# Attention probabilities left unnormalised; reciprocal row sums go through DRAM as rows and scale the z gates on GpSimd

## The chip, the core and the metric

The kernel runs on one core of a Trainium2 chip. The metric is the device time of one execution in microseconds. A core has these engines, each with a queue of its own that it works through in order: TensorE (PE in the profile, PEld for its weight loads), VectorE (DVE), ScalarE (ACT), GpSimd (POOL) and SyncE (SP). SP, ACT and POOL also issue the DMA transfers; a DMA that has to wait for something waits on its engine's queue, and all that stands behind it there waits too.

## What is computed

Two layers of a hybrid trunk over 512 tokens behind 16 learned meta tokens, 1024 channels wide. Each layer has a pooling branch and an attention branch with 8 heads of 96 query and 64 value channels. Only the attention branch is touched. Cut to that:

```
q, k, v  = projections of the layer's input, normalised, with rotary positions
s        = q @ k.T / sqrt(96), causal
p        = softmax(s)
o        = p @ v
y_mla    = (o * silu(z_mla)) @ mla_w_up
x        = x + (sigmoid(g_pool) * y_pool + sigmoid(g_mla) * y_mla) @ w_out
```

`silu(z_mla)` multiplies `o` element by element, so a factor that belongs to a query row of a head can stand on `p`, on `o`, or on the gate of z.

## The kernel before

Activations stand with channels on partitions and tokens along the free axis, `[128, 528]` a tile (16 meta tokens, then 512). Each product of float32 matrices is made of three matmuls in a faster format: weights and activations are split into a high and a low part, and high by high, high by low and low by high are summed (`mm3`, lines 188, 191, 192). The split of a weight tile is one ScalarE and one VectorE instruction (`wload`, lines 183 and 184: `whi`, `wlo`).

The main stream of weight products is a generator (`stream`), advanced by `step`. The attention heads are written between its pieces: `fill` and `gap` let so many nanoseconds of the stream pass by an own clock, and `after(ns, fn)` puts a piece of work off until that clock has gone on by `ns`; `LAG` is 2000. From this program order the scheduler of the build makes the order on each engine. So a change at one head moves instructions of the stream against those of the heads.

One head in `go` consists of these steps.

- `prep` makes its keys. VectorE multiplies the one half (line 849), POOL the other (line 850, `tmp<-kp,bc`); then `split` makes `kh` on ScalarE (line 297) and `kl` on VectorE (line 298). Part of the queries is made by lines 856 and 857.
- `head` makes the scores of four blocks of 128 queries in PSUM (`S`), takes their maximum on VectorE (line 879), and the exponentials with their row sums `rs` on ScalarE (line 886). Lines 918 and 919 finish the sum of the longest block and take the reciprocals. Then POOL multiplies the exponentials by these, for each of four blocks the 16 meta columns into `pm` (line 924) and the others in place (line 926), in `pa` and two `cq` tiles.
- `pv`, called for the head before, transposes the probabilities on PE (line 946, against the identity `cst`), splits them into `th` and `tl`, and multiplies by the values into `o` (lines 951 and 952). Two heads make a pair. At a pair's second head the meta columns of both are split on ScalarE and VectorE (lines 939 to 941, `pmr`) and transposed (line 957, against `identr`), and ScalarE copies that to `racc` (line 960).
- `part2`, put off by `2 * LAG` (3 for the last pair), adds the meta tokens' part by a matmul (line 974, `racc` by `vb`), multiplies by the z gate (line 982 in the first layer, a line like it in the last), and splits the result into `ogs`, the input of the products with `mla_w_up` (`mu`).

A layer's heads run beside the gates' weight products. POOL also issues accumulating DMAs that add up pairs of weight tiles for later (`weight_sums`, line 353, `wsum` and `wsumgp`), some of them between the heads. The z gates `zms` stand in `u` tiles. `tmp` is a pool of three buffers that almost all short-lived results share, among them the first stage of the gates (line 715) and the sum over a pair of heads, which keeps one until `part2` is through.

Of the kernel before, what the change touches and what calls it, by code (L numbers as in the profile page):

```python
# [9 lines left out]
F32 = mybir.dt.float32  # L10
# [3 lines left out]
AF = mybir.ActivationFunctionType  # L14
# [4 lines left out]
P = 128  # L19
DEPTH = 2  # L20
D = 1024
SEQ = 512
NM = 16
T = SEQ + NM
# [16 lines left out]
MT_ZM = 24  # L41
MT_GM = 28

C_ID, C_MASK = 0, 128
C_IK, C_IR = 256, 272
C_KPE, C_CQ = 284, 292
C_MM, C_VBD, C_INVF, C_CNT = 300, 316, 324, 325
N_CONST = 389

G_H, G_CKV, G_CQ, G_QN, G_QR, G_KN, G_KR, G_PS = 0, 8, 10, 16, 17, 18, 19, 20  # L50
# [4 lines left out]
LAG = 2000.0  # L55
# [17 lines left out]
def trunk(ctx, tc, xT, pos, win, wkr, wqb, wkb, wvb, wgr, wpu, wmu, wout, gains, const, yT):  # L73
# [26 lines left out]
    def mmt():  # L100
        return pp.tile([P, 512], F32, tag="mm", name=nm("mm"), bufs=4)
# [4 lines left out]
    FULL = [(0, HALF), (HALF, T)]  # L106
    XTOK = [(NM, T)]

    cst = cp.tile([P, N_CONST], F32, name="cst")
    gn = cp.tile([P, DEPTH * N_GAIN], F32, name="gn")  # L110
    xb = cp.tile([P, 8, W], F32, name="xb")
    early = []
# [17 lines left out]
    act.activation(warm, warm, AF.Copy)  # L130
    posb = slot("u3", I32)
    ident = cst[:, C_ID:C_ID + P]
    ones = cp.tile([P, P], F32, name="ones")
    dve.memset(ones, 1.0)
    wps = pp.tile([P, 512], F32, tag="o", name="wps", bufs=1)
    for i in range(WARM):
        pe.matmul(wps[:, 0:P], ones, ones, start=True, stop=True)
    maskw = cp.tile([P, 512], BF16, name="maskw")
    gp.memset(maskw[:, :512 - P], 0.0)
    identr = cp.tile([P, P], F32R, name="identr")  # L140

    def other_loads(made):
        for k, m in ((2, 0), (4, 1), (6, None)):
            ins = sp.dma_start(xb[:, k:k + 2, :T], xT[:, k:k + 2, :])
            behind(ins, made)
            if m is not None:
                raw = rawt()
                behind(sp.dma_start(raw, win[0, MT_CKV + m, :, 512:1024]), made)
                early.append(raw)
        behind(sp.dma_start(cst, const), made)  # L150
        behind(sp.dma_start(posb[:, :T], pos.partition_broadcast(P)), made)
        dve.tensor_copy(maskw[:, 512 - P:], cst[:, C_MASK:C_MASK + P])
        dve.tensor_copy(identr, ident)

    tcos, tsin = slot("tc")[:, :T], slot("ts")[:, :T]
# [105 lines left out]
    def after(ns, fn):  # L261
        pend.append((clk[0] + ns, fn))
        pend.sort(key=lambda e: e[0])
# [32 lines left out]
    def split(hi, lo, src, a, b):  # L296
        act.activation(hi[:, a:b], src, AF.Copy)  # L297
        dve.tensor_sub(lo[:, a:b], src, hi[:, a:b].bitcast(F32))  # L298
# [28 lines left out]
    scr = dp.tile([P, 8, SEQ], F32, name="scr")  # L327
    ndr = [[dp.tile([1, T], F32, name=f"ndr{l}{i}") for i in range(2)] for l in range(DEPTH)]
    ksr = [dp.tile([H, T], F32, name=f"ksr{l}") for l in range(DEPTH)]
    kdr = [dp.tile([H, T], F32, name=f"kdr{l}") for l in range(DEPTH)]  # L330

    wsum = {n: [dp.tile([P, 4, 512], F32, name=f"wsum{n}{u}") for u in range(k)] for n, k in (("gp", 4), (0, 2), (1, 2))}
# [26 lines left out]
    class Layer:  # L359
# [503 lines left out]
        def head(self, h, kq, prev, between):  # L863
            kh, kl, qh, ql = kq
            odd = h % 2
            nqs, hold = self.nqs, h == 0
            pa = slot("pa", bufs=2, w=416)
            pb = slot(f"cq{8 + odd}")
            pc = slot(f"cq{10 + odd}")
            bia = sm.tile([P, 5], F32, tag="bia", name=nm("bia"), bufs=2)  # L870
            rs = sm.tile([P, 5], F32, tag="rs", name=nm("rs"), bufs=2)

            def scores(i, out, a, b):
                q0 = NM + P * i
# [12 lines left out]

            pt = [pa[:, 0:144], pa[:, 144:416], pb[:, 0:400], pc[:, 0:T]]
            sa = sct()
            s1, s3 = sa[:, 0:272], sa[:, 272:272 + SPL]  # L890
            scores(1, s1, 0, 272)
            scores(3, s3, 0, SPL)
            top(1, 1, s1, causal(272))
            top(3, 4, s3, maskw[:, 0:SPL])
            sb = sct()
            s2 = sb[:, 0:400]
            scores(2, s2, 0, 400)
            if not self.last:
# [12 lines left out]
            scores(0, s0, 0, 144)  # L911
            top(3, 3, s4, causal(T - SPL))
            top(0, 0, s0, causal(144))
            dve.tensor_tensor(out=bia[:, 3:4], in0=bia[:, 3:4], in1=bia[:, 4:5], op=ALU.min)
            expo(3, 4, s3, pt[3][:, 0:SPL])
            expo(3, 3, s4, pt[3][:, SPL:T])
            expo(0, 0, s0, pt[0])
            dve.tensor_add(rs[:, 3:4], rs[:, 3:4], rs[:, 4:5])
            dve.reciprocal(rs[:, 0:4], rs[:, 0:4])  # L919
            if odd == 0:  # L920
                self.pm = sm.tile([P, 4, 32], F32, tag="pm", name=nm("pm"), bufs=2)
            for i in range(4):
                n = pt[i].shape[1]
                gp.tensor_mul(self.pm[:, i, 16 * odd:16 * odd + 16], pt[i][:, 0:NM],  # L924
                              rs[:, i:i + 1].to_broadcast([P, NM]))
                gp.tensor_mul(pt[i][:, NM:], pt[i][:, NM:], rs[:, i:i + 1].to_broadcast([P, n - NM]))  # L926
            return h, pt, self.pm

        def pv(self, prev, js):
            if prev is None:  # L930
                return
            h, pt, pm = prev
# [9 lines left out]
            for j in js:  # L942
                n = SEQ - P * j
                tr = mmt()
                for i in range(j, 4):
                    pe.transpose(tr[:, P * (i - j):P * (i - j + 1)], pt[i][:, NM + P * j:NM + P * (j + 1)], ident)  # L946
# [20 lines left out]
            dve.tensor_add(op, ops[n0:n0 + 64, :], op)  # L967
            if odd == 1:
                op = self.op
                mt = self.mt  # L970

                def part2():
                    th, m = mt, mmt()
                    pe.matmul(m, self.vb[:, P * p:P * (p + 1)], th[0:96, 0:512], start=True, stop=True)
                    self.ogs[p] = (slot(f"q{p}", F32R), slot(f"kn{p}", F32R))
                    f = op[:, NM:T]
                    dve.tensor_add(f, m, f)
                    if self.last:
                        dve.scalar_tensor_tensor(out=f, in0=f, scalar=0.5, in1=self.zms[p][:, NM:T],
                                                 op0=ALU.mult, op1=ALU.mult)  # L980
                    else:
                        dve.tensor_mul(f, f, self.zms[p][:, NM:T])
                    split(*self.ogs[p], f, NM, T)

                after((3 if p == 3 else 2) * LAG, part2)

        def meta_queries(self):
            smeta = self.smeta
            mxm = sm.tile([NM, 8], F32, tag="mxm", name=nm("mxm"))
# [404 lines left out]
```

## Time and profile before

| | us |
|---|---|
| median of 3 runs | 786.61 |
| lowest, highest | 786.53, 788.80 |
| the profiled execution | 785.38 |
| its span in the profile | 783.4 |

The span goes from the first instruction to the last; the execution's time has some 2.0 us more around it. Layer 0's heads lie at about 190 to 330 us of the span, layer 1's at 590 to 720. In the rows below, `out<-in` are the program's tiles without their numbers, `x` stands ahead of a count, and a group's row has its busy time, the mean of one in nanoseconds, and the idle time of its engine just before it with what ended it. Rows of the timeline begin with the start and the length in microseconds. In rows of the waits, the numbers are the total, the times and the longest. Rows of DMAs have the size of one and the median time from its issue until it has landed.

### The profile page before, as it was taken

The page shows a single profiled execution, that of the slowest core. Times are in us where ns is not written, and L with a number is a line of the kernel's source. Part 1 is how long each engine was busy: PE and PEld are TensorE (multiplying, and loading weights), DVE is VectorE, ACT ScalarE, POOL GpSimd, SP SyncE. Part 2 cuts the span into 40 slices and gives each one's busy share as a digit, 9 for nine tenths or more (in the row PEclk, how much of TensorE's full clock was granted, in tenths as well). Part 3 has the DMA queues.
Part 4 walks back from the last instruction along what each step waited for, and adds up shares of the span by engine and source line. Part 5 has one row for each costly group of instructions (what it writes and reads, how often), then busy time and mean ns, then how long its engine had stood idle before and what let it go on. Part 6 is the DMA issues. An engine that isn't in the chain of part 4 may idle for free.

```text
span 783.4 us, 15391 instructions
## 1 busy us (share of the span) xinstructions
PE 774.6 (99%) x5493; PEld 712.5 (91%) x5493; DVE 592.2 (76%) x1329; ACT 443.6 (57%) x1007; POOL 222.5 (28%) x310
## 2 busy tenths in 40 slices
PE   9999999999999999999999999999999999999998
PEld 8999899999999999999997898887788999887887
DVE  5848788447778977689875487775998899874995
ACT  8645645645556665544654356555657676764451
POOL 1024515203434332211110145131016334440211
PEclk9999999999999999999999999999999999999999
DMA  6242357765645465565533422425446666562751
GB/s 244 82 100 86 104 156 172 178 159 134 145 121 137 120 136 146 135 185 168 167 108 95 96 88 87 134 88 168 135 129 162 167 164 169 154 221 74 225 166 68
DMA packets 63005, 109.16 MB, mean 139 GB/s; under 512 B 10368, under 2 KB 14592, under 8 KB 62928
## 3 DMA queue, kind: packets, MB, share of 16 engines
q1 hardware_dynamic: 54640, 89.76, 38.1%
q0 software_dynamic: 7280, 16.59, 11.3%
q10 hardware_dynamic: 1008, 1.84, 0.6%
q8 instruction: 43, 0.70, 0.4%
q14 instruction: 34, 0.28, 0.1%
HBM read 100.18 MB, written 22.62 MB: 157 GB/s over the span
## 4 chain that ended last, share of the span: by engine, by line
PE 86%; DVE 5%; DMA 5%; issue 2%; ACT 1%; POOL 0%; ACTq 0%; DVEq 0%
PE mm L188 25%; PE mm L192 24%; PE mm L191 24%; PE S L191 2%; PE S L192 2%; PE S L188 2%; PE mm L946 2%; DVE wlo L184 2%; PE o L952 1%; PE o L951 1%; DMA raw<-wsumgp 1%; PE S L500 1%; DMA raw<-win 1%; PE mm L402 1%; DMA wsum<-wsum 1%
## 5 line engine op out<-in xcount | busy, mean ns | idle before, releaser
L188 PE MATMUL mm<-hh,whi 128*128 128x264 f32 (+2 forms) x1000 | 306.9, 310 | 1.1 <-DVE tmp L637 0.6
L191 PE MATMUL mm<-hl,whi 128*128 128x264 f32 (+2 forms) x1000 | 305.4, 307 | 0.0
L192 PE MATMUL mm<-hh,wlo 128*128 128x264 f32 (+2 forms) x1000 | 305.2, 308 | 0.2 <-DVE wlo L184 0.2
L184 DVE TENSOR_TENSOR wlo<-raw,whi 128x512 fp32r<-128x512 f32 (+2 forms) x261 | 189.4, 729 | 92.0 <-ACT whi L183 88.0
L183 ACT ACTIVATE whi<-raw 128x512 fp32r<-128x512 f32 (+2 forms) x261 | 156.3, 602 | 157.8 <-PE mm L191 93.0
L188 PEld LDWEIGHTS mm<-hh,whi 128*128 128x128 f32 x1000 | 187.5, 188 | 11.9 <-DVE tmp L637 0.8
L191 PEld LDWEIGHTS mm<-hl,whi 128*128 128x128 f32 x1000 | 188.2, 188 | 8.8
L192 PEld LDWEIGHTS mm<-hh,wlo 128*128 128x128 f32 x1000 | 187.2, 188 | 9.3 <-DVE wlo L184 1.2
L188 PE MATMUL mm<-cq,whi 128*128 128x264 f32 (+2 forms) x156 | 48.6, 312 | 0.9 <-ACT whi L183 0.9
L192 PE MATMUL mm<-cq,wlo 128*128 128x264 f32 (+2 forms) x156 | 48.0, 310 | 0.6 <-DVE wlo L184 0.6
L191 PE MATMUL mm<-cq,whi 128*128 128x264 f32 (+2 forms) x140 | 43.4, 311 | 0.0
L879 DVE CUSTOM_DVE_ANT_0 S<-S,maskw,nqs 128x288 f32<-128x288 f32 (+4 forms) x80 | 38.4, 496 | 2.5 <-PE S L192 2.2
L702 POOL TENSOR_TENSOR racc<-racc,tmp 128x264 f32<-128x264 f32 (+1 forms) x15 | 14.2, 948 | 85.1 <-ACT tmp L701 85.0
L188 PE MATMUL mm<-u,whi 128*128 128x264 f32 (+1 forms) x108 | 35.3, 326 | 0.1
L192 PE MATMUL mm<-u,wlo 128*128 128x264 f32 (+1 forms) x108 | 34.8, 322 | 0.0
L298 DVE TENSOR_TENSOR tl<-mm,th 128x512 fp32r<-128x512 f32 (+1 forms) x64 | 29.2, 480 | 7.3 <-ACT th L297 6.2
L850 POOL TENSOR_TENSOR tmp<-kp,bc 64x528 f32<-64x528 f32 x16 | 25.8, 1614 | 28.0 <-issue 13.7
L926 POOL TENSOR_TENSOR cq<-cq,rs 128x384 f32<-128x384 f32 (+1 forms) x32 | 33.4, 1043 | 0.0
L353 POOL DMA_DIRECT2D wsum<-wout x8 | 6.9, 863 | 89.2 <-PE mm L192 83.8
L188 PEld LDWEIGHTS mm<-cq,whi 128*128 128x128 f32 x156 | 29.4, 188 | 2.6 <-ACT whi L183 1.1
L192 PEld LDWEIGHTS mm<-cq,wlo 128*128 128x128 f32 x156 | 29.4, 188 | 2.6 <-DVE wlo L184 1.1
L924 POOL TENSOR_TENSOR pm<-pa,rs 128x16 f32<-128x16 f32 x32 | 11.4, 357 | 70.6 <-DVE rs L919 64.8
(342 smaller groups left out, 1699.7 us busy)
## 6 DMA issues: line engine op xcount, KB each, us to landing
raw<-win SPq DMA_DIRECT2D x139, 256.0 KB, 3.0
raw<-wout SPq DMA_DIRECT2D x22, 256.0 KB, 3.3
bc<-kdr SPq DMA_DIRECT2D x16, 264.0 KB, 4.2
wsum<-wout SPq DMA_DIRECT2D x16, 256.0 KB, 3.5
raw<-wpu SPq DMA_DIRECT2D x16, 256.0 KB, 3.2
wsumgp<-win SPq DMA_DIRECT2D x16, 256.0 KB, 3.3
raw<-wmu SPq DMA_DIRECT2D x16, 256.0 KB, 2.7
raw<-wsumgp SPq DMA_DIRECT2D x16, 256.0 KB, 3.5
```

The lines of the kernel that those rows point to most:

```text
L183: act.activation(hi[:, :n], raw[:, :n], AF.Copy)
L184: dve.tensor_sub(lo[:, :n], raw[:, :n], hi[:, :n].bitcast(F32))
L188: first = pe.matmul(out, wh, xh, start=start, stop=False, skip_group_check=more)
L191: pe.matmul(out, wh, xl, start=False, stop=False, skip_group_check=more)
L192: newest[0] = pe.matmul(out, wl, xh, start=False, stop=stop, skip_group_check=more)
L298: dve.tensor_sub(lo[:, a:b], src, hi[:, a:b].bitcast(F32))
L702: self.acc_last = gp.tensor_add(self.acc[:, a:b], self.acc[:, a:b], t[:, :b - a])
L850: gp.tensor_mul(kf[r0:r0 + 64, :], self.kp[r0:r0 + 64, :], bc[r0:r0 + 64, :])
L879: dve.tensor_tensor_reduce(out=sv, in0=sv, in1=mask, scale=nqs[:, i, h:h + 1], scalar=3e38, op0=ALU.add, op1=ALU.min, accum_out=bia[:, c:c ...
L924: gp.tensor_mul(self.pm[:, i, 16 * odd:16 * odd + 16], pt[i][:, 0:NM], rs[:, i:i + 1].to_broadcast([P, NM]))
L926: gp.tensor_mul(pt[i][:, NM:], pt[i][:, NM:], rs[:, i:i + 1].to_broadcast([P, n - NM]))
L946: pe.transpose(tr[:, P * (i - j):P * (i - j + 1)], pt[i][:, NM + P * j:NM + P * (j + 1)], ident)
```

## The change

The exponentials are no longer normalised. Of line 924 the copies of the meta columns to `pm` are left, without the factor; line 926 is gone. The row sums of both heads of a pair stand in one tile; at the pair's second head one reciprocal makes `rp`, `[128, 8]`: two heads by four blocks of queries. In `pv` of that head a new function `spread_rows` transposes `rp` on PE to 8 rows of 128, copies these by ScalarE, writes them by a DMA from ScalarE's queue to a DRAM tile `den`, so that each head has a row of 512, and reads them back by two DMAs from POOL's queue, each spread over 64 partitions, into `rows`. In `part2` POOL multiplies the z gate by `rows` ahead of the rest. `part2` is put off by one `LAG` more.

`rows` needs room in SBUF. So the constants' tile loses the mask's 128 columns, which now go through a `tmp` buffer, and `ones` is 32 columns wide in place of 128; the first matmuls, which only warm PE, take another `tmp` buffer.

```diff
-C_ID, C_MASK = 0, 128
+C_ID, C_MASK = 0, 261
...
-    cst = cp.tile([P, N_CONST], F32, name="cst")
+    cst = cp.tile([P, C_MASK], F32, name="cst")
...
-    ones = cp.tile([P, P], F32, name="ones")
-    dve.memset(ones, 1.0)
+    ones = cp.tile([P, 32], F32, name="ones")
+    warmer = tmp()[:, 0:P]
+    dve.memset(warmer, 1.0)
...
-        behind(sp.dma_start(cst, const), made)
+        behind(sp.dma_start(cst, const[:, 0:C_MASK]), made)
+        tri = tmp()[:, 0:P]
+        behind(sp.dma_start(tri, const[:, C_MASK:C_MASK + P]), made)
...
+    den = [[dp.tile([2, SEQ], F32, name=f"den{l}{p}") for p in range(4)] for l in range(DEPTH)]
...
-            rs = sm.tile([P, 5], F32, tag="rs", name=nm("rs"), bufs=2)
+            if odd == 0:
+                self.rs = sm.tile([P, 2, 5], F32, tag="rs", name=nm("rs"), bufs=2)
+            rs = self.rs[:, odd, :]
...
             dve.tensor_add(rs[:, 3:4], rs[:, 3:4], rs[:, 4:5])
-            dve.reciprocal(rs[:, 0:4], rs[:, 0:4])
             if odd == 0:
-                self.pm = sm.tile([P, 4, 32], F32, tag="pm", name=nm("pm"), bufs=2)
-            for i in range(4):
-                n = pt[i].shape[1]
-                gp.tensor_mul(self.pm[:, i, 16 * odd:16 * odd + 16], pt[i][:, 0:NM],
-                              rs[:, i:i + 1].to_broadcast([P, NM]))
-                gp.tensor_mul(pt[i][:, NM:], pt[i][:, NM:], rs[:, i:i + 1].to_broadcast([P, n - NM]))
+                self.pm = sm.tile([P, 4, 32], F32, tag="pm", name=nm("pm"))
+            else:
+                self.rp = sm.tile([P, 8], F32, tag="mxm", name=nm("rp"))
+                dve.reciprocal(self.rp.rearrange("p (a b) -> p a b", a=2), self.rs[:, :, 0:4])
+            for i in (1, 2, 3, 0):
+                gp.tensor_copy(self.pm[:, i, 16 * odd:16 * odd + 16], pt[i][:, 0:NM])
             return h, pt, self.pm
+
+        def spread_rows(self, p, tr):
+            pe.transpose(tr[0:8, 384:512], self.rp, ident)
+            t, d = tmp(), den[self.l][p]
+            act.activation(t[0:8, 0:P], tr[0:8, 384:512], AF.Copy)
+            act.dma_start(d.rearrange("a (b c) -> (a b) c", c=P), t[0:8, 0:P])
+            self.rows = slot("rows", w=SEQ)
+            for o in range(2):
+                gp.dma_start(self.rows[64 * o:64 * o + 64, :], d[o:o + 1, :].partition_broadcast(64))
...
+                if odd == 1 and j == 1:
+                    self.spread_rows(p, tr)
                 split(th, tl, tr[:, :n], 0, n)
...
-                mt = self.mt
+                mt, rows = self.mt, self.rows
 
                 def part2():
+                    z = self.zms[p][:, NM:T]
+                    gp.tensor_mul(z, z, rows)
                     th, m = mt, mmt()
...
-                after((3 if p == 3 else 2) * LAG, part2)
+                after((4 if p == 3 else 3) * LAG, part2)
```

More of the change, by code (lines that the diff above doesn't have):

```diff
@@ L42 @@
 MT_GM = 28
-C_ID, C_MASK = 0, 128
-C_IK, C_IR = 256, 272
-C_KPE, C_CQ = 284, 292
-C_MM, C_VBD, C_INVF, C_CNT = 300, 316, 324, 325
+C_ID, C_MASK = 0, 261
+C_IK, C_IR = 128, 144
+C_KPE, C_CQ = 156, 164
+C_MM, C_VBD, C_INVF, C_CNT = 172, 188, 196, 197
 N_CONST = 389
@@ L132, in trunk @@
     ident = cst[:, C_ID:C_ID + P]
-    ones = cp.tile([P, P], F32, name="ones")
-    dve.memset(ones, 1.0)
+    ones = cp.tile([P, 32], F32, name="ones")
+    warmer = tmp()[:, 0:P]
+    dve.memset(warmer, 1.0)
     wps = pp.tile([P, 512], F32, tag="o", name="wps", bufs=1)
     for i in range(WARM):
-        pe.matmul(wps[:, 0:P], ones, ones, start=True, stop=True)
+        pe.matmul(wps[:, 0:P], warmer, warmer, start=True, stop=True)
     maskw = cp.tile([P, 512], BF16, name="maskw")
     gp.memset(maskw[:, :512 - P], 0.0)
+    gp.memset(ones, 1.0)
     identr = cp.tile([P, P], F32R, name="identr")
@@ L149, in other_loads @@
                 early.append(raw)
-        behind(sp.dma_start(cst, const), made)
+        behind(sp.dma_start(cst, const[:, 0:C_MASK]), made)
+        tri = tmp()[:, 0:P]
+        behind(sp.dma_start(tri, const[:, C_MASK:C_MASK + P]), made)
         behind(sp.dma_start(posb[:, :T], pos.partition_broadcast(P)), made)
-        dve.tensor_copy(maskw[:, 512 - P:], cst[:, C_MASK:C_MASK + P])
+        dve.tensor_copy(maskw[:, 512 - P:], tri)
         dve.tensor_copy(identr, ident)
@@ L983, in part2 @@
                     split(*self.ogs[p], f, NM, T)
-                after((3 if p == 3 else 2) * LAG, part2)
+                after((4 if p == 3 else 3) * LAG, part2)
         def meta_queries(self):
             smeta = self.smeta
-            mxm = sm.tile([NM, 8], F32, tag="mxm", name=nm("mxm"))
+            mxm = sm.tile([P, 8], F32, tag="mxm", name=nm("mxm"))[0:NM, :]
             bc = lambda t: t.unsqueeze(2).to_broadcast([NM, 8, NM])
```

## The prediction

> **What bounds the kernel now.** I read the share of busy time first, then the chain of waits, then the stretches in which the changed code runs, then who waits for whom, and last the few microseconds around one head.
>
> ```profile
> PE 774.6 (99%) x5493; PEld 712.5 (91%) x5493; DVE 592.2 (76%) x1329; ACT 443.6 (57%) x1007; POOL 222.5 (28%) x310
> ```
>
> ```profile
> PE 86%; DVE 5%; DMA 5%; issue 2%; ACT 1%; POOL 0%; ACTq 0%; DVEq 0%
> ```
>
> ```profile
> 190.00:330.00 140.00, 140.00 (x1140) 138.44 (x1139) 110.29 (x274) 84.06 (x218) 54.74 (x84) 1.00 0.55 134
> 330.00:340.00 10.00, 9.86 (x80) 9.60 (x80) 6.80 (x21) 3.85 (x11) 0.60 (x1) 1.00 0.70 161
> 590.00:720.00 130.00, 128.74 (x829) 115.17 (x828) 107.10 (x248) 84.79 (x213) 51.70 (x76) 1.00 0.60 165
> ```
>
> The first line and the chain agree: TensorE is the bound, and POOL, on which most of the change lies, has none of the chain. The windows (length, then busy time of PE, PEld, DVE, ACT, POOL, granted clock, DMA share, GB/s) are the stretches of the two layers' heads. PE is idle 0.00 + 0.14 + 1.26 = 1.40 us in them. That is all a pure relief of other engines can give back by this measure; 774.6 us of matmuls stay. The clock is 1.00 in all three, so it is no term. Nothing ahead of the heads changes its order on PE.
>
> The waits name POOL only as what others wait for:
>
> ```profile
> ACT pmr L939 <- POOL pm L924: 12.2, 8, 3.0
> ACT kh L297 <- POOL tmp L850: 7.9, 5, 3.1
> PE mm L188 <- DVE tmp L637: 0.6, 1, 0.6
> ```
>
> ScalarE waits for POOL 12.2 us in eight waits for the meta columns and 7.9 us in five for the key multiply of L850 (columns: total, times, longest). The third line is the longest kind of PE wait in layer 1's heads, 0.6 us. So POOL's lateness reaches PE only where ScalarE's and VectorE's own slack has run out. One such place is in the chain of layer 1:
>
> ```profile
> 635.19 0.79 POOL cq L926
> 636.19 0.32 ACT pmr L939
> 636.53 0.77 DVE pmr L940
> 637.30 0.33 DVE sv L627
> 638.49 0.68 DVE wlo L184
> 639.21 0.38 PE mm L192
> ```
>
> **The change part by part.** *Removed:* the normalising multiplies on POOL.
>
> ```profile
> L926 POOL TENSOR_TENSOR cq<-cq,rs 128x512 f32<-128x512 f32 x16 | 18.0, 1122 | 0.0
> L926 POOL TENSOR_TENSOR cq<-cq,rs 128x384 f32<-128x384 f32 x16 | 15.4, 964 | 0.0
> L924 POOL TENSOR_TENSOR pm<-cq,rs 128x16 f32<-128x16 f32 x32 | 13.0, 407 | 0.0
> L926 POOL TENSOR_TENSOR pa<-pa,rs 128x256 f32<-128x256 f32 x16 | 11.5, 717 | 0.0
> L661 POOL TENSOR_TENSOR q<-tmp 128x512 f32<-128x512 f32 x2 | 2.3, 1164 | 0.1
> L534 POOL TENSOR_TENSOR q<-q,tc 128x512 f32<-128x512 f32 x2 | 3.6, 1784 | 5.1 <-DVE tmp L532 5.1
> L1091 POOL DMA_DIRECT2D xb<-xT x8 | 4.4, 554 | 23.4 <-DVE cq L1052 16.9 <-DVE cq L1049 6.5
> ```
>
> The first four rows are 57.9 us; the two kinds left out (128x16 and 128x128 of `pa`) are smaller. Against them stand 64 copies of 128x16 (at most the 407 ns of the multiply of that size, 26 us), eight multiplies of 128x512 with both inputs full width (between 1164 and 1784 ns by the last two multiplies above, so 9 to 14 us) and 16 DMA issues (554 ns each, 9 us). POOL does less, but it was idle 72% of the span; PE gets at most the 1.40 us. The chain at 635 us dissolves, since the meta copies no longer queue behind wide multiplies; the other idle pieces hang on VectorE's own queue. I take half: **-0.7 us**, between 0 and -1.4. Eight reciprocals less on VectorE lie inside that.
>
> *Added on PE:* eight transposes of `rp`, one a pair.
>
> ```profile
> 214.75 0.27 PE L946 MATMUL mm<-cst,pa 128*128 128x128 f32 x1
> 214.86 0.38 PE L946 MATMUL mm<-cst,cq 128*128 128x128 f32 x2
> ```
>
> Here one 128x128 transpose starts 0.11 us after another. The new one streams the same 128 columns, with 8 weight columns. It stands between the transposes and the meta matmuls. PE after the change, second head of a pair (`rp` holds the reciprocals, `pmr` the meta columns):
>
> ```order
> L961 MATMUL mm_3128<-cst,pa_2786 128x128
> L961 MATMUL mm_3128<-cst,cq_501_2787 128x128
> L961 MATMUL mm_3128<-cst,cq_502_2788 128x128
> L936 MATMUL mm_3128<-cst,rp_2924 8x128
> L974 MATMUL mm_3145<-identr,pmr_3113 96x128 x4
> L192 MATMUL S_3184<-kh_2977,qhl_107 128x288
> ```
>
> Before, `identr` followed the transposes directly. PE is the bound, so nothing hides it: 8 x 0.11 = **+0.9 us**; half or double that are the bounds, 0.4 to 1.8.
>
> *Added on POOL's queue:* two DMAs and a multiply that wait for a round trip through DRAM. What is queued behind them counts. POOL before, at the third head of layer 0 (`tmp` is the key multiply for the next head):
>
> ```order
> L924 TENSOR_TENSOR pm_3189<-cq_547_3040,rs_3043 128x16
> L926 TENSOR_TENSOR cq_547_3040<-cq_547_3040,rs_3043 128x384
> L924 TENSOR_TENSOR pm_3189<-cq_548_3041,rs_3043 128x16
> L926 TENSOR_TENSOR cq_548_3041<-cq_548_3041,rs_3043 128x512
> L850 TENSOR_TENSOR tmp_3251<-kp_976,bc_2725 64x528
> ```
>
> and now:
>
> ```order
> L942 DMA rows_3138<-den_123 64x512 x2
> L932 COPY pm_3198<-cq_550_3044 128x16
> L932 COPY pm_3198<-pa_3042 128x16
> L991 TENSOR_TENSOR u_475_2646<-u_475_2646,rows_3138 128x512
> L855 TENSOR_TENSOR tmp_3256<-kp_988,bc_2732 64x528
> ```
>
> The z multiply moved in front of the key multiply: whatever holds up `rows` holds up the next head's keys, and so its scores on PE. In the other pairs the key multiply stands ahead of the DMA issues or many microseconds behind the z multiply; in the second pair of each layer it stands behind the issues alone, which wait for the write. The time before at the place above:
>
> ```profile
> 217.95 0.63 ACT L856 ACTIVATE qhl<-q 64x528 fp32r<-64x528 f32 x1
> 226.70 1.31 POOL L850 TENSOR_TENSOR tmp<-kp,bc 64x528 f32<-64x528 f32 x1
> 228.04 0.65 ACT L297 ACTIVATE kh<-tmp 128x528 fp32r<-128x528 f32 x1 [3.10 <-POOL tmp L850]
> 228.72 0.71 DVE L298 TENSOR_TENSOR kl<-tmp,kh 128x528 fp32r<-128x528 f32 x1 [2.35 <-ACT kh L297]
> 229.49 0.47 PE L188 MATMUL S<-kh,qhl 128*128 128x272 f32 x2
> ```
>
> There is no slack: ScalarE sat 3.10 us for POOL, and the scores began 0.06 us after `kl` ended (228.72 + 0.71). Now the new chain. ScalarE issues the write behind the `qhl` copy, so at about 218.6 + 0.3 us for the extra 8x128 copy. Round trips of this kind:
>
> ```profile
> 92.00 2.98 DMA ksr<-tmp
> 95.00 1.66 DMA ka<-ksr
> xb<-xT POOLq DMA_DIRECT2D x8, 264.0 KB, 3.9
> scr<-xb POOLq DMA_DIRECT2D x8, 132.0 KB, 2.4
> wsum<-wout POOLq DMA_DIRECT2D x8, 256.0 KB, 6.1
> ```
>
> With 1.7 to 3.0 us for the write (the two small transfers), 2 x 0.55 us of issue on POOL, 2.4 to 3.9 us until the second 128 KB have landed, 1.2 to 1.8 us for the z multiply and 1.31 us for the key multiply, the key multiply ends between 218.9 + 7.7 = 226.6 and 218.9 + 11.1 = 230.0, against 228.0 before. One matmul of the stream follows another after 0.12 us:
>
> ```profile
> 261.80 0.28 PE L188 MATMUL mm<-hh,whi 128*128 128x264 f32 x1
> 261.92 0.28 PE L191 MATMUL mm<-hl,whi 128*128 128x264 f32 x1
> ```
>
> On PE the first scores with `kh` now stand 14 matmuls earlier in the order, 1.7 us, so at 229.5 - 1.7 = 227.8; with 0.65 us for `kh` the key multiply has to end by 227.1. The stall is 0 to 2.9 us; I take **+1.3 us**, a little under the middle, since plain transfers of half the size should land nearer to 2.4 than to 3.9.
>
> The DMA page of the Trainium skill, "DMA: Bandwidth & Descriptors", section "Anatomy of one DMA — SWDGE (gpsimd) path", gives a fixed 2.0 us plus the bytes over 436e3 for such a transfer. For 128 KB that would be an estimated 2.3 us, near the low end of the rows, the key multiply would end at about 227.5 and the sum come out at 787.5. The 264 KB row is at 3.9 us where the formula makes 2.6, so the trace does not bear it out here.
>
> *Added by the buffer:* the 8x128 copy takes one of the three `tmp` buffers until its DMA has landed. VectorE, second pair of layer 0, with the waits (DMAHW0 is that landing):
>
> ```order
> L302 TENSOR_TENSOR tl_3669<-mm_3664,th_3668 128x384 [waits Activation_49]
> L722 SCALAR_TENSOR_TENSOR xb<-tmp_3712,xb 128x264 [waits Activation_49]
> L720 TENSOR_TENSOR tmp_3728<-mm_3628,rinv_492 128x264 [waits DMAHW0_49,PE_49]
> L854 TENSOR_TENSOR tmp_3784<-kn_197_1137,bc_3257 64x528 [waits DVE_49]
> L188 TENSOR_TENSOR wlo_3819<-raw_3816,whi_3818 128x512 [waits DMAHW4_49,Activation_49]
> ```
>
> Before, the third row waited for PE and VectorE alone. VectorE runs in this order, so a late landing holds up the keys and the weights behind it.
>
> ```profile
> 255.26 0.43 DVE L715 TENSOR_TENSOR tmp<-mm,rinv 128x264 f32<-128x264 f32 x1
> 259.19 0.69 DVE L298 TENSOR_TENSOR kl<-tmp,kh 128x528 fp32r<-128x528 f32 x1
> 262.16 0.29 PE L188 MATMUL S<-kh,qhl 128*128 128x272 f32 x1
> ```
>
> The landing comes 1 to 2 us after 255.3; `kl` ended 2.28 us ahead of the scores that need it. That covers it, and the key multiply behind the DMA issues of this pair too, just so. A like wait stands once in layer 1, where VectorE is busy 107.10 of 130. I take **+0.3 us**, between 0 and 2.
>
> *At no cost:* the split load of the constants and the smaller `ones` (used long after the first stage); the later due time of the pair's last step, because from the `rp` transposes to the multiply by z lie 15 to 26 us of matmuls for seven pairs and 11 for the last (their places in PE's order, counted at 0.12 us for 264 columns), against a chain of 7.7 to 11.1 us. If that cover were gone at the last pair, 1 to 2 us. The 2 MB more of DMA are 2% of 109 MB.
>
> **Sum:** -0.7 + 0.9 + 1.3 + 0.3 = +1.8 us on the profiled span of 783.4 us, so 785.2. That execution took 785.38 us, 2.0 more than its span, and the median of the three runs shown is another 1.2 higher: 786.61 + 1.8 = **788.4 us**.
>
> **The rivals.** *Slower: the round trip is dear and POOL's queue hands it to PE.* If the POOL DMAs land like `wsum` (6.1 us, the last row of that fence) the key multiply ends at up to 232.2, the stall is 5.1 us, and VectorE's buffer wait takes its 1 to 2. It decides from a landing of about 4 us on. Price 0.9 + 4 + 1 - 0.7 = +5.2 with a landing between, 791.8. For it: POOL's queue already shows 5 to 6 us. Against: those are accumulating transfers of double size; plain ones take 2.4 to 3.9.
>
> *Faster: VectorE gets free.* VectorE's subtraction of two SBUF tiles is longer where POOL is busy:
>
> ```profile
> L184 DVE TENSOR_TENSOR wlo<-raw,whi 128x512 fp32r<-128x512 f32 x22 | 15.1, 685 | 1.0 <-ACT whi L183 0.7
> L184 DVE TENSOR_TENSOR wlo<-raw,whi 128x512 fp32r<-128x512 f32 x47 | 36.5, 779 | 10.1 <-ACT whi L183 9.7
> ```
>
> The first row is 340 to 410 us, with hardly any POOL work, the second 590 to 720. 47 x 0.094 = 4.4 us of VectorE could come back in layer 1. If PE got all its idle 1.40 us, and 2 us more from matmuls that now issue late without showing as idle, it would be -3.4 + 0.9 = -2.5: 784.1. Against: VectorE is not full, and PE waited for it 0.6 us at most. The Trainium skill's page "SBUF — State Buffer", section "SBUF: two separate sides", says that a VectorE operation with two SBUF inputs and a GpSimd operation that reads SBUF lock each other out; the two rows agree.
>
> *The rows come late at the last pair*, and VectorE waits there with the weights of the next stage behind: +2 us on the forecast, 790.4.
>
> **Chances.** Forecast 0.50 (its own range 786.4 to 789.6), dear round trip 0.30, VectorE free 0.16, last pair 0.04. 0.3% of 786.61 is 2.4 us, about what a measurement of this kernel can tell from no change. Of the forecast 0.07 lies beyond it on the slow side, of the dear trip 0.02 within it and of the free VectorE 0.02. So faster 0.14, same 0.47, slower 0.39. The range goes from the faster case to that of the dear trip, 784.2 to 791.8.
>
> **What would show it.** Right: the key multiply of layer 0's fourth head begins after the first z multiply, ScalarE's wait for `kh` is longer than 3.1 us there, and PE shows a wait for `kh` near 228 us; the waits of `pmr` for POOL are gone; eight `rp` transposes about 0.11 us apart from their neighbours. Wrong: `rows` landing in under 2.4 us or over 4 us; a layer-1 stretch shorter by over 2 us; PE waiting in places where neither `rows` nor `den` is due.

## The result and the profile after

| | before | after |
|---|---|---|
| median of 6 runs, us | 786.37 | 790.23 |
| lowest to highest, us | 785.43 to 788.80 | 789.10 to 792.44 |
| profiled execution (its span), us | 785.38 (783.4) | 790.71 (788.6) |

The ratio is 1.0053, with a 95% interval from 1.0040 to 1.0067: 3.1 to 5.3 us slower. The predicted 788.4 us was 1.8 low; the range of 784.2 to 791.8 holds the time, the forecast's own range (to 789.6) misses it by 0.6. Of the prediction's three cases "same", within 0.3%, had the largest chance (0.47); "slower" (0.39) is what came.

The page of the changed kernel, share of busy time and chain by engine:

```profile
PE 775.5 (98%) x5501; PEld 713.0 (90%) x5501; DVE 588.9 (75%) x1321; ACT 443.8 (56%) x1015; POOL 184.5 (23%) x271
...
PE 84%; DMA 6%; DVE 5%; issue 2%; ACT 2%; DVEq 0%; ACTq 0%; SPq 0%
```

PE's busy time grew by 0.9 us, about what the eight transposes would ask, and POOL lost 38 us. The span grew by 5.2, so the rest is PE standing still. The windows say where (length, busy time of PE, PEld, DVE, ACT, POOL, granted clock, DMA share, GB/s):

```profile
190.00:330.00 140.00, 140.00 (x1137) 138.12 (x1136) 108.72 (x269) 83.69 (x221) 35.05 (x60) 1.00 0.58 140
...
590.00:720.00 130.00, 125.56 (x816) 112.80 (x815) 103.17 (x242) 84.83 (x221) 31.32 (x55) 1.00 0.62 169
```

Layer 0's heads, where the prediction put its largest loss, have no idle PE at all. In layer 1's heads PE is idle 4.44 us in place of 1.26. Who PE waits for in the whole kernel (engine and line, released by; total, times, longest):

```profile
PE mm L196 <- DVE wlo L188: 2.9, 2, 2.2
PE mm L192 <- ACT whi L187: 2.0, 2, 1.5
PE o L969 <- DVE tl L302: 1.3, 3, 0.7
```

No row names POOL, `rows` or `den`. (Lines have shifted by 4 or more: 184 is now 188, 192 is 196, 850 is 855.) The place of the predicted stall, around the third head of layer 0, in the timeline (start, length, engine, line):

```profile
219.33 1.11 POOL L942 DMA_DIRECT2D rows<-den  x2 [1.85 <-DMA den<-tmp]
...
222.87 1.60 POOL L991 TENSOR_TENSOR u<-u,rows 128x512 f32<-128x512 f32 x1 [2.10 <-DMA rows<-den]
224.84 1.33 POOL L855 TENSOR_TENSOR tmp<-kp,bc 64x528 f32<-64x528 f32 x1 [0.37 <-DVE xb L722]
...
226.84 0.65 ACT L301 ACTIVATE kh<-tmp 128x528 fp32r<-128x528 f32 x1 [0.77 <-DVE tmp L854]
...
228.31 0.47 PE L192 MATMUL S<-kh,qhl 128*128 128x272 f32 x2
```

The key multiply does stand behind the z multiply, as forecast, but it ends at 226.2 us, below even the low end of the estimate (226.6), and `kh` waited last for VectorE's half of the keys. The start makes the difference, not the length of the chain. The prediction had ScalarE issue the write behind the `qhl` copy, at 218.9 us; it was issued at 217.38:

```profile
217.38 0.55 ACTq L939 DMA_DIRECT2D den<-tmp  x1
...
218.42 0.63 ACT L861 ACTIVATE qhl<-q 64x528 fp32r<-64x528 f32 x1
```

In the order of ScalarE's program the write does stand behind that copy. But the issue went out 1.0 us before the `qhl` copy began, and right after the 8x128 copy of the reciprocals (217.10 to 217.35), which it needs. From the write's issue to the end of the key multiply it is 8.8 us, inside the 7.7 to 11.1 of the prediction.

The largest new stall is in layer 1's second pair. The chain of waits there, then VectorE's and POOL's timeline:

```profile
641.75 2.43 DMA den<-tmp
...
644.27 0.13 DVE tmp L642
...
644.62 0.16 DVE rs L925
...
644.80 0.54 DVE tmp L854
...
645.53 2.88 DVE wlo L188 x2
...
648.46 0.50 PE mm L196
```

```profile
644.27 0.42 DVE L642 TENSOR_TENSOR tmp<-mm,sv 128x256 f32<-128x256 f32 x1 [0.64 <-DMA den<-tmp]
644.62 0.15 DVE L925 TENSOR_TENSOR rs<-rs 128x1 f32<-128x1 f32 x1
644.80 0.70 DVE L854 TENSOR_TENSOR tmp<-kn,bc 64x528 f32<-64x528 f32 x1
645.53 2.87 DVE L188 TENSOR_TENSOR wlo<-raw,whi 128x512 fp32r<-128x512 f32 x2
```

```profile
644.78 1.13 POOL L942 DMA_DIRECT2D rows<-den  x2 [1.61 <-DMA den<-tmp]
645.90 1.34 POOL L855 TENSOR_TENSOR tmp<-kp,bc 64x528 f32<-64x528 f32 x1
647.15 0.70 POOL L932 COPY pm<-pa 128x16 f32<-128x16 f32 x1
```

VectorE first waits 0.64 us for a `tmp` buffer that the write of `den` holds. Then two `wlo`, 0.69 us each where POOL is quiet, take 2.87 together, and they meet POOL's key multiply of 1.34 us. PE needs them: it stood still for 2.2 us. The kernel before has that same key multiply, beside VectorE's work at the same place:

```profile
643.62 1.79 POOL L850 TENSOR_TENSOR tmp<-kp,bc 64x528 f32<-64x528 f32 x1 [6.47 <-DVE rs L918]
```

```profile
643.53 0.69 DVE L184 TENSOR_TENSOR wlo<-raw,whi 128x512 fp32r<-128x512 f32 x1
644.25 1.72 DVE L849 TENSOR_TENSOR tmp<-kn,bc 64x528 f32<-64x528 f32 x1
```

There VectorE's half of the keys is stretched to 1.72 us, and PE was not waiting for it; `wlo` had gone ahead. So at this place the two kernels do not differ in whether POOL holds up VectorE but in which instruction it meets. That is a matter of order, and the scheduler of the build had made another order: against the kernel before, some 370 of PE's matmuls and 180 of VectorE's instructions stand at another place, counted as the fewest moves that turn the one order into the other.

### The profile page after: what moved, and what is told of

It reads as the page before. It is cut to its first block, busy times and chain, and to the rows that moved or that the text cites. A ratio compares the mean times of both kernels' runs of the same rounds, so it can differ in the third digit from the quotient of the medians.

```text
span 788.6 us, 15365 instructions
## 1 busy us (share of the span) xinstructions
PE 775.5 (98%) x5501; PEld 713.0 (90%) x5501; DVE 588.9 (75%) x1321; ACT 443.8 (56%) x1015; POOL 184.5 (23%) x271
## 4 chain that ended last, share of the span: by engine, by line
PE 84%; DMA 6%; DVE 5%; issue 2%; ACT 2%; DVEq 0%; ACTq 0%; SPq 0%
PE mm L192 24%; PE mm L196 24%; PE mm L195 24%; DMA raw<-win 2%; PE S L195 2%; PE S L196 2%; PE S L192 2%; DVE wlo L188 2%; PE mm L961 2%; PE o L969 1%; ACT whi L187 1%; PE o L968 1%; PE S L505 1%; DMA raw<-wqb 1%; PE mm L407 1%
## 5 line engine op out<-in xcount | busy, mean ns | idle before, releaser
L196 PEld LDWEIGHTS mm<-hh,wlo 128*128 128x128 f32 x1000 | 187.1, 188 | 11.2 <-DVE wlo L188 3.0
L886 DVE CUSTOM_DVE_ANT_0 S<-S,maskw,nqs 128x400 f32<-128x400 f32 (+4 forms) x80 | 38.3, 498 | 3.5 <-PE S L196 3.2
L893 ACT ACTIVATE cq<-S,bia 128x400 f32<-128x400 f32 (+2 forms) x48 | 24.6, 515 | 15.3 <-DVE bia L921 8.4
L195 PE MATMUL mm<-kn,whi 128*128 128x264 f32 (+1 forms) x96 | 30.5, 320 | 0.0
L196 PE MATMUL mm<-q,wlo 128*128 128x264 f32 (+1 forms) x96 | 30.2, 321 | 0.0
L192 PE MATMUL mm<-q,whi 128*128 128x264 f32 (+1 forms) x96 | 29.6, 323 | 0.5 <-ACT q L301 0.5
```

The lines of the kernel that those rows point to most:

```text
L192: first = pe.matmul(out, wh, xh, start=start, stop=False, skip_group_check=more)
L195: pe.matmul(out, wh, xl, start=False, stop=False, skip_group_check=more)
L196: newest[0] = pe.matmul(out, wl, xh, start=False, stop=stop, skip_group_check=more)
```

## The experiments

The theory that came out of the traces: the change by itself costs about its transposes, and most of the loss is the new order (*order theory*). The rivals were the `tmp` buffer, the lock-out of VectorE by POOL's new work, the transposes themselves, and the later due time. All ratios are to the kernel before on the same chip.

### Parts, with the order left to the scheduler

**own_buffer.** The copy of the reciprocals goes into the tile that the rows fill later.

```diff
-            t, d = tmp(), den[self.l][p]
+            d = den[self.l][p]
+            self.rows = t = slot("rows", w=SEQ)
```

> The changed kernel with the 8x128 copy of the reciprocals put into the rows tile (which its own transfer fills later) instead of one of the three tmp buffers; nothing else. Buffer theory (the wait of VectorE for a tmp buffer that the den write holds costs 0.6 us or more at the second pair of layer 1 and like places): 788.2 to 789.4 us against 790.2 for the change, and no wait of VectorE's tmp for DMA den. Lock-out theory (VectorE's wlo is slowed by GpSimd's work, the buffer is nothing): 789.8 to 790.4.

Measured: 789.35 us, ratio 1.0047 (1.0034 to 1.0061). In microseconds that is inside the buffer theory's range, but the kernel before took 784.99 us on this chip, so the ratio decides: 1.0047 of the 786.4 us of the result is 790.1, in the range of the lock-out theory. The wait of `tmp` for `den` is gone, and the time is hardly less: 0.0006 between the two ratios is inside both intervals. The stall of 2.2 us is gone from the trace too (PE waits 1.0 us for `wlo` in place of 2.9), but PE was still idle 3.02 us in layer 1's heads (126.98 busy of 130), and at 760 us, where the change stands still for 1.50 us, it does so for 1.93. The edit moved some 50 of PE's matmuls against the change. So the buffer alone is not where the loss lies.

**no_rows.**

```diff
-                if odd == 1 and j == 1:
-                    self.spread_rows(p, tr)
...
-                    gp.tensor_mul(z, z, rows)
```

> The changed kernel without the transposes of rp, the write, the row loads and the z multiply: the output lacks the normalisation. What is left is the pure relief of POOL and VectorE and the later due time. Round-trip theory (all of the loss is in what was added: transposes 0.9, rows and z multiply on GpSimd, buffer): 785.6 to 786.6 us, 0 to 0.8 below the kernel before. Order theory (the later due time or the moved meta copies cost on their own): 787.5 to 789. Freed VectorE (rival of the prediction): below 785.

Measured: 785.22 us, ratio 1.0002 (0.9992 to 1.0012). All added work is out, 53 us of POOL's are saved, and nothing is gained. That is about what the round-trip theory says (0 to 0.8 us below the kernel before), and not the 1 us and more above it of the order theory. Read alone, it puts the whole loss on the added work and nothing on the relief; but it has the later due time and another order in it (some 330 of PE's matmuls moved against the kernel before, some 110 against the change), so it parts neither.

**transposes.** The kernel before, and in `pv` at the pair's second head:

```diff
+                if odd == 1 and j == 1:
+                    pe.transpose(tr[0:8, 384:512], cst[:, C_IK:C_IK + 8], ident)
```

> The kernel before with eight more transposes of eight columns (of a constant tile), one a pair, at the place where the change has those of rp; nobody reads them. The prediction's term of +0.9 us: 787.3 us. Rivals: the transpose is hidden behind PE's waits, 786.4 to 786.7; or it costs its whole record of 0.27 us, +2.2, 788.6.

Measured: 788.94 us, ratio 1.0053 (1.0041 to 1.0066). Eight instructions that nobody reads cost as much as the whole change. By PE's own record they cannot: its busy time went up from 774.6 to 775.4. But 40 of PE's matmuls and 30 of VectorE's instructions stand elsewhere, most of PE's in layer 1's heads, where PE is now idle 2.89 us.

**later_due.** The kernel before with one number changed:

```diff
-                after((3 if p == 3 else 2) * LAG, part2)
+                after((4 if p == 3 else 3) * LAG, part2)
```

> The kernel before with the pair's last step due one LAG later (3 and 4 instead of 2 and 3), nothing else. The prediction took this at no cost: 786.2 to 786.8 us. Order theory: the shifted weight splits and the later ogs cost 1 us or more, 787.4 to 788.5.

Measured: 794.99 us, ratio 1.0127 (1.0104 to 1.0150). The same instructions in another order (some 220 of PE's matmuls and 130 of VectorE's moved) cost 8 to 12 us, more than twice the change. Within the change the same edit came along with +0.5% or, in no_rows, with nothing. The due time acts on the program's order alone, so what it costs here can't be told without the order that it brings.

### The same with the order held

To take the order out, the instructions that both kernels have were tied to the order that they have in the kernel before, on all five engines: each to its forerunner on the same engine, by an edge that orders the issue and makes nobody wait. In every program below with `_held` in its name, none of these instructions stands at another place than before.

```python
for run in runs:                       # one list for each engine, from the kernel before
    for a, b in zip(run, run[1:]):
        tc.add_manual_dep(made[b], made[a].name, NoSync)
```

**transposes_held.** As transposes; the eight are the only difference in any queue.

> The kernel before with the same eight unread transposes, but with the order of every other instruction on every engine held to that of the kernel before (edges between neighbours on one engine, no waits); the kernel with free order took 1.0053 of the time before. Order theory (the build's scheduler moves some forty matmuls and thirty VectorE instructions when it sees the transposes, and that costs the rest): ratio 1.0005 to 1.002, the +0.9 us of the prediction's term. Rival (a transpose with eight columns costs PE half a microsecond each by itself): ratio 1.004 to 1.006 again.

Measured: 787.51 us, ratio 1.0011 (0.9996 to 1.0026). This is +0.9 us, the term, and it excludes 1.0053: four fifths of the loss that the transposes brought was the order. The interval reaches zero, and the page shows PE busy for 774.6 us, as before, so the size of the term rests on the median alone.

**change_held.** The whole change, with three adjustments without which the order could not be kept: staging as in own_buffer, reciprocals in the tile of the sums, and the old due time.

```diff
-                self.rs = sm.tile([P, 2, 5], F32, tag="rs", name=nm("rs"), bufs=2)
+                self.rs = sm.tile([P, 10], F32, tag="rs", name=nm("rs"), bufs=2)
...
-                self.rp = sm.tile([P, 8], F32, tag="mxm", name=nm("rp"))
-                dve.reciprocal(self.rp.rearrange("p (a b) -> p a b", a=2), self.rs[:, :, 0:4])
+                dve.reciprocal(rs[:, 0:8], rs[:, 0:8])
+                self.rp = rs[:, 0:8]
...
-                after((4 if p == 3 else 3) * LAG, part2)
+                after((3 if p == 3 else 2) * LAG, part2)
```

> The whole change, with the order of all instructions that both kernels have held to that of the kernel before on all five engines. For that the pair's last step has its old due time again, the 8x128 copy is staged in the rows tile and the reciprocals stand in the rs tile. Order theory: the change by itself costs the transposes less some relief, ratio 0.9995 to 1.0025 (786 to 788 us by 786). Rival (row loads, the z multiply in GpSimd's queue and its lock-out of VectorE stall PE by themselves): ratio 1.004 or more, with PE waiting for wlo or the z multiply in layer 1.

Measured: 786.66 us against 786.97 for the kernel before, ratio 0.9995 (0.9982 to 1.0009). In the old order the change, so adjusted, costs nothing that can be measured. Layer 1's heads in its windows:

```profile
590.00:720.00 130.00, 128.87 (x836) 116.02 (x835) 105.68 (x251) 87.06 (x227) 34.41 (x57) 1.00 0.64 174
```

PE is idle 1.13 us, against 1.26 before and 4.44 in the change.

**change_due_back.** The program of change_held with its order left free, so that nothing but the order lies between the two.

> The same program as change_held with the order left to the scheduler: the change with its own staging place and the old due time. Order theory: its order is another one again, so its time differs from change_held by 1 us or more, mostly upward: ratio 1.003 to 1.012. Rival (the later due time, which holds a tmp buffer 2 us longer, makes the loss): ratio at most 1.002.

Measured: 788.67 us, ratio 1.0028 (1.0011 to 1.0045), against 0.9995: the intervals do not meet, so the order of one and the same program is worth 0.0033, 2.6 us. (The ratio is just under the 1.003 that was expected, and its interval still takes in the rival's 1.002.) What lies between 1.0028 and the 1.0053 of the change is the later due time, the `tmp` buffer, the tile of the reciprocals and the order that these bring; no run parts them. Its stall stands in layer 1's second pair again, without any wait for `den`:

```profile
645.93 1.55 DVE L926 TENSOR_TENSOR rs<-rs 128x1 f32<-128x1 f32 x1
647.40 0.68 DVE L188 TENSOR_TENSOR wlo<-raw,whi 128x512 fp32r<-128x512 f32 x1
```

```profile
646.11 1.34 POOL L855 TENSOR_TENSOR tmp<-kp,bc 64x528 f32<-64x528 f32 x1
```

An addition of 128 numbers, 0.15 us elsewhere, took 1.55 us until the key multiply was over, and `wlo`, which PE needed, stood behind it.

**relief_held.** change_held without transposes, write, row loads and z multiply.

> As change_held, but without the transposes, the write, the row loads and the z multiply, so the output lacks the normalisation: the relief alone, in the order of the kernel before. The prediction's term for it is -0.7 us, between 0 and -1.4: ratio 0.998 to 1.000. Rival (VectorE freed is worth more): below 0.9975.

Measured: 783.32 us (6 runs), ratio 0.9947 (0.9929 to 0.9966), 2.7 to 5.6 us less than before. By these times the relief is worth several times the term of -0.7 once the order is kept. In layer 1's heads PE is busy 129.63 of 130. That is 0.9 us less idle time than before. The profiled execution was the longest of the six (785.21 us), and its span is the 783.4 us of the kernel before; but at 190 us, ahead of the heads, PE is 15 matmuls behind (1517 against 1532, 186.63 us busy against 188.28). So from there on it gains some 1.7 us. Where the rest comes from the trace does not show.

**no_z_held.** change_held without the line `gp.tensor_mul(z, z, rows)`.

> change_held without GpSimd's z multiplies; the rows are loaded and not used, so the output lacks the normalisation. Between change_held (0.9995) and relief_held (0.9947) lie the transposes (0.0011) and 0.0037 for write, row loads and z multiply. Lock-out theory (GpSimd's wide reads slow VectorE's wlo from 0.69 to over 1.1 us, and PE waits for it): most of the 0.0037 comes back, ratio 0.9955 to 0.9975. Rival (transfers and issues on the queues make it, or it is the spread between executions): 0.9985 to 1.0000.

Measured: 786.17 us, ratio 1.0003 (0.9989 to 1.0017), against 0.9995 with the z multiplies. That is beside the rival's range and far from the theory's, so lock-out by the z multiply falls: eight wide multiplies less on POOL gave PE nothing. Between this kernel and relief_held lie the transposes (0.0011) and the write with its copy and the row loads; 0.0045 with an uncertainty of about 0.003 remains for the latter. No run parts them, and relief_held has half as many executions as the others.

### Looking for a version that beats both

**z_dve_held.** change_held with `dve.tensor_mul(z, z, rows)`.

> change_held with the z multiply on VectorE (0.7 us each, eight of them) instead of GpSimd. Lock-out theory: VectorE gains as much from GpSimd's silence (1.3 us of overlap at each) as it pays, ratio 0.9985 to 1.0000, GpSimd's key multiplies earlier. Rival (VectorE's own load is what PE waits for in layer 1, each 0.7 us there goes to PE at least in half): 1.001 to 1.004.

Measured: 798.63 us, ratio 1.0165 (1.0146 to 1.0184), much worse than either theory allowed. VectorE's waits show why:

```profile
DVE u L992 <- DMA rows<-den: 13.8, 6, 3.5
```

The multiply stands where VectorE gets to it before the rows have landed, and all the rest of VectorE's queue waits with it. PE's longest wait, 4.5 us, leads in the chain of waits back over a weight load and a `wlo` to one of these landings. In the change POOL waits 19.7 us for the rows, in time that it has, and no wait of PE names that.

**direct_held.** No transposes and no copy; the write itself turns the reciprocals.

```diff
-            pe.transpose(tr[0:8, 384:512], self.rp, ident)
-            act.activation(t[0:8, 0:P], tr[0:8, 384:512], AF.Copy)
-            act.dma_start(d.rearrange("a (b c) -> (a b) c", c=P), t[0:8, 0:P])
+            act.dma_start(d.rearrange("a (b c) -> c (a b)", c=P), self.rp)
```

> change_held with the transposes, their PSUM columns and ScalarE's copy taken out: the reciprocals (128x8) are written to DRAM in transposed order straight from the rs tile, element by element, and the rows are loaded as before. The transposes cost +0.9 us by the prediction's term and by transposes_held (ratio 1.0011); if that write lands in the 15 us and more that the z multiply has, the ratio is 0.9970 to 0.9990, a gain on both kernels. Rival (the write of 1024 single elements is so slow, 10 us or more, that rows, z multiply and the key multiply behind it come late): 1.001 or more, with PE waiting for kh or for the last step.

Measured: 834.83 us, ratio 1.0629 (1.0609 to 1.0649). In the list of DMA issues (each 4 KB, median time to landing) and in the chain of waits after one of them:

```profile
den<-rs ACTq DMA_DIRECT2D x8, 4.0 KB, 11.2
```

```profile
246.10 13.39 DMA raw<-win
```

The write of 1024 single numbers takes 11.2 us, and a weight load beside it 13.39 us where the median of these loads in this run is 3.5. In the chain of waits three more of the eight writes have such a load beside them, of 11.71, 12.45 and 13.15 us. The rival had named the late rows; that the weights are held up too it had not.

**dve_transposed_held.** The turning on VectorE, the write in rows of 128 bytes on SyncE's queue.

```diff
+                dve.reciprocal(self.rows[:, 0:32].rearrange("p (a b) -> p a b", a=4),
+                               rs[:, 0:8].unsqueeze(1).to_broadcast([P, 4, 8]))
+                dve.transpose(self.rows[:, 32:64], self.rows[:, 0:32])
...
+            for k in range(4):
+                sp.dma_start(d.rearrange("a (b k i) -> k (a b) i", b=4, i=32)[k], t[32 * k:32 * k + 8, 32:64])
```

> change_held without PE's transposes and ScalarE's copy, in the order of the kernel before: VectorE writes the reciprocals of a pair four times side by side into the rows tile (128x32) and turns them in blocks of 32x32; four small transfers of 8x32 on SyncE's queue bring them to DRAM in rows of 128 bytes; row loads and z multiply as in the change. Theory (the transposes cost PE 0.9 us, the rest lies beside other work, and relief_held's gain is partly kept): ratio 0.9965 to 0.9990, faster than both kernels. Rival (SyncE's four extra issues a pair delay the weights behind them, or the small write lands as late as the element-wise one): 1.001 or more, with PE waiting for whi or wlo behind a late raw.

Measured: 790.11 us, ratio 1.0048 (1.0031 to 1.0064). The chain of waits in layer 1's third pair:

```profile
671.15 5.77 DMA rows<-den
...
677.09 1.28 POOL u L992
678.37 1.45 POOL tmp L855
...
679.84 0.64 ACT kh L301
```

and of PE's waits there:

```profile
PE o L969 <- ACT th L301: 2.4, 1, 2.4
```

This is the stall that the prediction had put into layer 0 of the change: rows late (5.77 us), z multiply, key multiply behind it, `kh` and what is behind it on ScalarE late, among it `th`, for which PE stood still 2.4 us. Neither rival of the expectation had it. POOL's new instructions were not held, since the kernel before has none like them, and here the row loads and the z multiply came to stand ahead of that key multiply.

No version that keeps the normalisation beat the kernel before; change_held equals it.

## Why the prediction was right, and where it was not

**The bound and what the transposes cost: right.** PE bounds the kernel before and the changed one (86% and 84% of the chain). +0.9 us for eight transposes is what transposes_held measures (1.0011), though its interval also reaches zero.

**The relief, -0.7 us, between 0 and -1.4: too small.** It was bounded by PE's visible idle time in the heads of one execution. relief_held measures -2.7 to -5.6. The profiled execution of before (785.38 us) is 1.0 us below the median of the result, so some idle time that other executions have may not have been in it; that is not enough for the difference. The trace of relief_held shows some 1.7 us of the gain, and where the rest comes from stays open. The sign that the prediction had named for this part came: `pmr` waits for POOL 12.2 us before and not at all in the change.

**The key multiply behind the z multiply, +1.3 us: the position was right, the price was nothing there.** The chain took 8.8 us, as long as was estimated, but it began 1.5 us sooner, because the write's issue did not wait for the `qhl` copy ahead of it; so the keys were there before PE came to the scores. Two of the signs that the prediction had named did not come: ScalarE's wait for the keys is 0.77 us there, not over 3.1, and PE has no wait near 228 us. The rows land in 2.8 to 6.0 us, median 3.1, over the whole kernel; the mechanism is real, as dve_transposed_held shows, but it strikes only where a late landing and a key multiply without slack meet.

**The `tmp` buffer, +0.3: seen, and not decisive.** The wait of 0.64 us is at the head of the largest stall; own_buffer took it away, and the time stayed within the error.

**The step that failed is the one that has no term.** The prediction noted that nothing ahead of the heads changes its order on PE, laid three pieces of the new order beside the old, and priced the instructions added and moved in them as if everything else stood still. That the scheduler moved hundreds of others in the heads was given no cost and no chance. The runs price it: 1.0053 against 1.0011 for the transposes free and held, 1.0028 against 0.9995 for one and the same program, 1.0127 for a due time alone. Of the 0.0053 of the change, 0.0033 is shown to be order alone, in the adjusted program.

With the order held that program comes to -0.4 us (0.9995 of 787), and by another sum than the prediction's +1.8: the transposes +0.9, the relief -4.2 (relief_held), and +2.9, with an uncertainty of some 2.2, that is left for the write, the row loads and the z multiply. The prediction had -0.7 for the second and +1.6 for the third. So it had both too small, if these differences of medians hold, and what the +2.9 are made of no run shows: PE's waits in change_held name neither `rows` nor `den`. By these ratios the added work costs about the same in both orders (0.0048 from relief_held to change_held, 0.0051 from no_rows to the change), and what the new order takes away is the gain of the relief (0.9947 held, 1.0002 free, there with the later due time).

With the order free the loss is 4.2 us, and PE's waits in it name neither the z multiply nor the rows. The range held by luck, because the dear round trip had been let in at +5.2 us: right size, wrong reason. What would be wrong by the prediction's own list did show up: PE waiting where neither `rows` nor `den` is due, for `wlo`, `whi` and `tl`.

**The rivals.** Dear round trip: by landings of up to 6.0 us it had its condition at places, but PE has no wait for it in the change. VectorE free: refuted for the change, where `wlo` of layer 1's heads has a mean of 799 ns against 779 before; in relief_held the mean is 747 and a gain of that size is there, but no trace shows it to be VectorE's. The Trainium skill's page "SBUF — State Buffer", section "SBUF: two separate sides", on which that rival leaned, has a VectorE operation with two SBUF inputs and a GpSimd operation that reads SBUF lock each other out; the traces agree in the single case (0.15 us became 1.55, and two `wlo` of 0.69 each became 2.87 together). The time does not follow from how much POOL works, since eight z multiplies more or less changed nothing that can be measured. Last pair late: not seen in the change; z_dve_held's waits for the rows are a thing of its own queue.

## What to carry to other kernels

When a build's scheduler sets the order, an edit is two edits: the work and the order. Tie the common instructions to the old order with edges that make nobody wait before a loss or a gain is put down to the work, and count how many instructions moved before pricing those that were added. In this kernel, whose bound engine is 99% busy, the second edit was the larger one: a due time alone was worth 1.3%.

## What the runs showed of the hardware beside this

**A short stall can cost more than its length.** In change_due_back PE stands still for 1.66 us up to 648.14 (from the end and start of the matmul records, as all stalls here). The windows on both sides of that point (the number after POOL's is the granted clock):

```profile
644.00:648.00 4.00, 2.43 (x17) 1.80 (x15) 3.94 (x6) 2.67 (x9) 3.14 (x5) 1.00 0.43 130
648.00:652.00 4.00, 3.86 (x10) 3.11 (x11) 3.94 (x8) 1.39 (x4) 1.83 (x2) 0.57 0.50 132
```

From 649 to 651 us the clock is 0.50. So 0.57 over 4 us is half speed for 3.4 us: another 1.7 us are lost, an estimate from these windows. The same comes with stalls of 1.93 us in own_buffer, 1.94 in later_due, 2.41 in dve_transposed_held and 2.38 in z_dve_held, though not after the 2.23 us in the profiled execution of the change or the 2.30 of direct_held, and after none of 1.0 to 1.6 us. Of the twelve executions of change_due_back the four longest (790.4 to 793.3 us) are those with a mean clock of 0.997 or less; the others have 0.998 to 1.0. So a part of the spread goes with this. The Trainium skill's page "TensorE: Matmul & The Clock Gate", section "Part 1: The HAM clock gate (the "warmup" mystery)", has the array go to half clock after an idle window of about 3.4 us that runs freely; the length of the slow piece agrees, but stalls of half that length were enough here.

**One write of single elements slows its neighbours:** 4 KB as 1024 numbers landed after 11.2 us, and four of the eight writes have a 256 KB weight load of 11.71 to 13.39 us beside them in the chain of waits (direct_held), where the median of the loads of `win` is 3.5.

**A DMA's issue can overtake its own engine's work.** In the change the write of `den` stands behind the `qhl` copy in ScalarE's program and was issued at 217.38 us, the copy began at 218.42: reading the start of the write off the order of the queue put it 1.5 us too late.
